# Copying a pass's results aside with GpSimd and storing them at the start of the next pass, in a softmax-times-V kernel

## The chip, the cores and the metric

The kernel runs on one core of one Trainium2 chip. The metric is the device time of one execution in microseconds (us), lower is better. The engines of the core are called PE (matrix multiplication; PEld is its loading of weights), DVE (VectorE), ACT (ScalarE), POOL (GpSimd) and SP (which here only issues the DMA transfers).

## The reference

For 8 x 12 = 96 heads of 1024 x 1024 scores and a 1024 x 64 matrix V, in float32:

```python
def reference(scores: np.ndarray, v: np.ndarray) -> np.ndarray:
    scores_max = np.max(scores, axis=-1, keepdims=True)
    attn = np.exp(scores - scores_max)
    attn = attn / (np.sum(attn, axis=-1, keepdims=True) + 1e-8)
    return np.matmul(attn, v).astype(np.float32)
```

The scores are 403 MB; V and the result are 25.2 MB each.

## The kernel before, in words

One loop runs over the 96 heads in 24 **passes** of four heads (`n0` = 0, 4, ... 92; below, pass p has n0 = 4p). A pass has two **halves**, k = 0 and k = 1, of two heads each. The body of the loop is written out once and used by all passes, with branches (`tc.If`) for the last three.

**A half.** The scores of two heads lie in `s_bufs[k]`: 128 partitions, 16 rows of 1024 scores on each, 8.39 MB. There are two such buffers, one for each half. The 16 rows are worked off in eight **turns** of two rows. ACT takes the exponential of two rows into one of the buffers `p_nat` (float16, L384; eight buffers). No maximum is subtracted; what that needs is verified on the side (`seen`, `watch_v`, `fold`, `judge`). PE transposes each row in eight 128 x 128 blocks into `psT` (L397, two buffers). DVE copies them to `pt` (L409 for two rows at once, L405 for one row in the turns called `late`: the second half of half 1). PE multiplies `pt` by `vones`, which is V with columns of ones (L152, eight products for a row), so that the sums of the softmax come out beside the products. After each three rows DVE takes the reciprocals (L132) and writes the scaled results to `out_bufs[k]` (L140). `in_line` fixes the order on PE: the products of a row follow the transposes of the row three later.

**End of a pass.** `fold` (two small DVE reductions, L284 and L285) reads the whole row of `seen`, in which the reciprocals and the result of `watch_v` lie. `watch_v` is one ACT instruction over the 1 MB of V of the next pass (L266); it writes one column of `seen`, and as a by-product `p_bufs[0]`. `spread_v` (POOL, L255, eight casts for each half) fills `vones` of one half from `v_sb`.

**The queue of transfers.** All transfers are issued by SP, and `queue` chains them, so that they are issued in the order of the program. In the passes 0 to 20 the order is: the load of half 0 of the next pass (`load_first`, issued when ACT has finished half 0), the store of half 0's results (`store(n0, 0)`, 0.52 MB), the load of half 1 of the next pass (when ACT has finished half 1), the store of half 1's results, the load of V for the pass after the next (1.05 MB). In the passes 21 and 22 the loads of scores are cut into parts, each issued when its own rows are free: (4, 6, 6) rows for half 0, and for half 1 (4, 4, 4), then the store of half 1, then (2, 1, 1). In pass 23 nothing is loaded; `end` stores half 1 in two pieces.

**How transfers report.** The build gives the transfers of the loop's body eight semaphores in turn, here called lanes 0 to 7 (`DMAHW0` to `DMAHW7`). Since all passes share one body, both sides of a branch count each lane up by the same amount, and a wait names a lane and a count.

Of the kernel before, what the change touches and what calls it, by code (L numbers as in the profile page):

```python
# [8 lines left out]
FP32 = mybir.dt.float32  # L9
FP16 = mybir.dt.float16  # L10
# [16 lines left out]
def kernel(  # L27
# [6 lines left out]
    nc = tc.nc  # L34
    P = 128

    B, H, SQ, SK = scores.shape
    Bv, Hv, SKv, D = v.shape
    assert (B, H, SK) == (Bv, Hv, SKv)
    BH = B * H  # L40
    assert SQ % P == 0 and SK % P == 0
    C = SK // P
    EB = 2
    G = 3
    LAG = 3
    AHEAD = 4
# [6 lines left out]
    T = 2  # L53
    K = AHEAD // T
    W = P // T
    R = SQ // W
# [8 lines left out]
    out_rows = out.rearrange("b h (j r) d -> (b h j) (r d)", j=W)  # L65

    const_pool = ctx.enter_context(tc.tile_pool(name="const", bufs=1))
    sb_pool = ctx.enter_context(tc.tile_pool(name="sbpool", bufs=1))
# [10 lines left out]
    def buffers(pool, count, shape, dtype, name):  # L79
        return [pool.tile(shape, dtype, name=f"{name}{k}") for k in range(count)]  # L80

    s_bufs = buffers(sb_pool, K, [P, R, SK], FP32, "s_nat")
    v_sb = sb_pool.tile([P, C // L, S, L, D], FP32, name="v_sb")
    p_bufs = buffers(sb_pool, 8, [P, EB, SK], FP16, "p_nat")
    pt_bufs = buffers(sb_pool, 2, [P, EB, SK], FP16, "pt")
    out_bufs = buffers(sb_pool, K, [P, R, D], FP32, "out_sb")
    small_pool = ctx.enter_context(tc.tile_pool(name="small", bufs=1))
    seen = small_pool.tile([P, 1 + K * R + 2], FP32, name="seen")
    nc.gpsimd.memset(seen, 1.0)
# [1 line left out]


    psO_bufs = buffers(ps_pool, 4, [P, 512], FP32, "psO")
    turn = {}

    def take(bufs):
        k = turn.get(id(bufs), 0)
        turn[id(bufs)] = k + 1
        return bufs[k % len(bufs)]

    pending = []
    queued = []
    line = []

    def after(a, b):

        tc.add_manual_dep(
            a.ins,
            b.ins.name,
            mybir.DependencyInfo(mybir.DependencyClass.NoSync, mybir.DependencyReason.DATA),  # L110
            reason="order",
        )

    def in_line(op):

        if line:
            after(op, line[-1])
        line.append(op)

    def queue(dma):  # L120

        if queued:
            after(dma, queued[-1])
        queued.append(dma)
# [37 lines left out]
        if r == R - 1 and k < K - 1:  # L162
            spread_v(k)

    def store(n0, k):

        to = out_rows.rearrange("(m x) y -> m x y", x=P)[bass.ds((n0 + T * k) // T, 1)]
        to = to.rearrange("o x y -> (o x) y")
        send(nc.sync.dma_start(out=to, in_=out_bufs[k][:].rearrange("x r d -> x (r d)")))

    def send(dma):
        for other in stores:
            apart(dma, other)
            apart(other, dma)
        apart(dma, dma)
        stores.append(dma)
        queue(dma)

    def end():

        cut = (GROUPS - 2) * G
        for a, b in ((0, cut), (cut, R)):
            send(
                nc.sync.dma_start(
                    out=out_rows[(BH - T) * W : BH * W, a * D : b * D],
                    in_=out_bufs[K - 1][:, a:b].rearrange("x r d -> x (r d)"),
                )
            )

# [3 lines left out]
    def apart(a, b, reason="stores of two heads are disjoint"):  # L193
        tc.declare_no_dep(a.ins, b.ins, across_iterations=True, reason=reason)
# [18 lines left out]
    def load(k, n, parts=(R,), r=0, **cond):  # L213
        rows_n = sc_rows[bass.ds(n // T, 1)].rearrange("o x r k -> (o x) r k")
        for rows in parts:
            queue(
                nc.sync.dma_start(  # L217
                    out=s_bufs[k][:, r : r + rows, :], in_=rows_n[:, r : r + rows, :], **cond
                )
            )  # L220
            r += rows

    def branch_at(op):

        after(op, line[-1])

    def load_first(n0):

        before = queued[-1:]
        n = (n0 + AHEAD) % BH  # L230
        with tc.If(n0 < BH - 3 * AHEAD) as cmp:
            load(0, n)
            branch_at(queued[-1])
        with cmp.Else():
            queued[:] = before
            load(0, n, (4, 6, 6), cond=(n0 < BH - AHEAD))
            branch_at(queued[-1])
        line.append(queued[-1])

    def load_v(n, **cond):  # L240

# [9 lines left out]
    def spread_v(k):  # L251

        for t in range(T):
            for s in range(S):
                nc.gpsimd.tensor_copy(  # L255
                    out=vones[s * Q : (s + 1) * Q, k, :, t, 0:D].rearrange(
                        "i (h l) d -> i h l d", l=L
                    ),
                    in_=v_sb[(k * T + t) * Q : (k * T + t + 1) * Q, :, s],
                )  # L260

    def watch_v():


        junk = p_bufs[0][:].rearrange("p r k -> p (r k)")
        return nc.scalar.activation(  # L266
            out=junk,
            in_=v_sb[:].rearrange("p h s l d -> p (h s l d)"),
            func=mybir.ActivationFunctionType.Abs,
            scale=1.0 / SUM_MAX,  # L270
            accum_out=seen[:, K * R + 1 : K * R + 2],
        )
# [78 lines left out]
    def last(n0, bank):  # L351

        before = queued[-1:]
        k = K - 1
        with tc.If(n0 < BH - AHEAD) as cmp:
            spread_v(k)
            n = (n0 + AHEAD + T * k) % BH
            with tc.If(n0 < BH - 3 * AHEAD) as cmp2:
                queued[:] = before
                load(k, n)  # L360
                store(n0, k)
                load_v((n0 + 2 * AHEAD) % BH)
            with cmp2.Else():
                queued[:] = before
                load(k, n, (4, 4, 4))
                store(n0, k)
                load(k, n, (2, 1, 1), 12)
                load_v(BH - AHEAD, cond=(n0 < BH - 2 * AHEAD))
        with cmp.Else():
            queued[:] = before  # L370
            end()
            judge(bank)

    def heads(n0):

        for k in range(K):
            st = dict(psO=[take(psO_bufs) for g in range(GROUPS)])
            for r in range(R):
                late = k == K - 1 and r >= R // 2
                if r % EB == 0:  # L380
                    p_nat, psT2, pt2 = take(p_bufs), take(psT_bufs), take(pt_bufs)
                    rows = 1 if late else EB
                    for g in range(0, EB, rows):
                        exp = nc.scalar.activation(  # L384
                            out=p_nat[:, g : g + rows, :].rearrange(
                                "p r (x v) -> p x r v", v=Q * L
                            ),
                            in_=s_bufs[k][:, r + g : r + g + rows, :].rearrange(
                                "p r (i x l) -> p x (r i) l", i=Q, l=L
                            ),  # L390
                            func=EXP,
                        )
                        rewrite(p_nat, exp)
                p_row = p_nat[:, r % EB, :].rearrange("p (h q l) -> p h l q", q=P, l=L)
                psT, pt = psT2[:, r % EB, :], pt2[:, r % EB, :]
                for c in range(C):
                    turned = nc.tensor.transpose(  # L397
                        out=psT[:, c * P : (c + 1) * P],
                        in_=p_row[:, c // L, c % L, :],
                        identity=ident16[:],  # L400
                    )
                    in_line(turned)
                    other_bank(psT2, r % EB, turned)
                if late:
                    copy = nc.vector.tensor_copy(out=pt, in_=psT)  # L405
                    rewrite(pt2, copy)
                    other_bank(psT2, r % EB, copy)
                elif r % EB == EB - 1:
                    copy = nc.vector.tensor_copy(out=pt2[:], in_=psT2[:])  # L409
                    rewrite(pt2, copy)  # L410
                if r == 6 and k == K - 1:
                    load_first(n0)
                    store(n0, 0)
                if r == 13 and k == K - 1:
                    with tc.If(n0 < BH - AHEAD):
                        watch = watch_v()
                        branch_at(watch)
                    line.append(watch)
                pending.append((n0, k, r, pt, st))
                while len(pending) > (LAG - 1 if late and r >= R - EB else LAG):  # L420
                    finish(pending.pop(0))
        while pending:
            finish(pending.pop(0))
        fold()
        last(n0, st["psO"][-1])
# [52 lines left out]
```

## Time and profile before

| | |
|---|---|
| three runs | 1065.42, 1064.98, 1064.54 us (median 1064.98) |
| the profiled execution | 1065.58 us |
| its span, from first to last instruction | 1063.8 us |
| busy, share of the span | PE 77%, PEld 74%, ACT 71%, DVE 66%, POOL 22% |
| DMA queue | 99.1% of the 16 engines' span; 453 MB at a mean of 426 GB/s |
| granted PE clock, mean | 0.875 |

The profiled execution took 1.78 us more than its span, and 0.60 us more than the median of the three runs. In the lists of groups and waits a row names a line of the kernel, an engine, what it writes and reads, and times; "A <- B: x, n, y" in the list of waits means that A waited for B x us in total, n times, at the longest y. In the timeline a row has the start in us from the start of the span, the length, the engine, the line and the instruction, and in brackets how long the engine had been idle and what ended that.

### The profile page before, as it was taken

How to read it: one execution, taken by the hardware profiler on the slowest of the kernel's cores; microseconds unless marked ns; L12 is line 12 of the kernel's file. 1: busy time of each engine (PE TensorE's matmuls, PEld its weight loads, DVE VectorE, ACT ScalarE, POOL GpSimd, SP SyncE). 2: the span in 40 equal slices, each digit the busy share in tenths (PEclk: the TensorE clock that was granted, in tenths of full speed). 3: DMA queues.
4: the chain of work that ended last, by engine and by line, in shares of the span. 5: the costliest groups of instructions: out<-in, count | busy, mean ns of one | idle time of the engine just before them, and what ended most of it. 6: DMA issues, size and time to landing. Idle time of an engine off the chain costs nothing. (4 is left out here: it accounts for less than half of the span.)

```text
span 1063.8 us, 33293 instructions
## 1 busy us (share of the span) xinstructions
PE 814.6 (77%) x12289; PEld 790.1 (74%) x12289; DVE 706.8 (66%) x1395; ACT 754.3 (71%) x530; POOL 239.0 (22%) x400
## 2 busy tenths in 40 slices
PE   2588778886877768886788778886788868887967
PEld 2488767786877768886777778876787867777967
DVE  1467766776667757676577765776667756677858
ACT  4477577776777667766777577775777667768965
POOL 3031130211312113112031130311312113112131
PEclk9788988888898978899888887998888898988989
DMA  9999999999999999999999999999999999999995
GB/s 394 435 429 431 414 434 453 414 453 430 418 453 414 432 455 414 453 414 432 452 416 451 407 443 451 416 448 427 426 448 419 423 437 441 414 453 413 430 415 228
DMA packets 19587, 453.04 MB, mean 426 GB/s; under 512 B 2176, under 2 KB 2304, under 8 KB 8960
## 3 DMA queue, kind: packets, MB, share of 16 engines
q1 hardware_dynamic: 19584, 452.99, 99.1%
q8 instruction: 3, 0.05, 0.0%
HBM read 437.26 MB, written 25.17 MB: 435 GB/s over the span
## 5 line engine op out<-in xcount | busy, mean ns | idle before, releaser
L384 ACT ACTIVATE p_nat<-s_nat 128x2048 f16<-128x2048 f32 (+1 forms) x480 | 707.1, 1557 | 292.5 <-DMA s_nat<-in_scores_dram 278.5
L397 PE MATMUL psT<-ident,p_nat 128*128 128x128 f16 x6144 | 525.5, 238 | 215.5 <-ACT p_nat L384 213.4
L397 PEld LDWEIGHTS <-p_nat 128*128 128x128 f16 x6144 | 442.3, 120 | 227.4 <-ACT p_nat L384 226.2
L409 DVE COPY pt<-psT 128x2048 f16<-128x2048 f16 x288 | 352.4, 1224 | 319.0 <-PE L152 159.0
L152 PE MATMUL psO<-vones,pt 128*128 128x130 f16 x6144 | 504.6, 229 | 28.4 <-DVE pt L405 17.7
L152 PEld LDWEIGHTS <-pt 128*128 128x128 f16 x6144 | 408.0, 102 | 40.7 <-DVE pt L405 21.9
L255 POOL CAST vones<-v_sb 32x512 f16<-32x512 f32 x392 | 238.1, 607 | 811.6 <-PE psT L397 360.9
L140 DVE TENSOR_TENSOR out_sb<-psO,seen 64x192 f32<-64x192 f32 (+1 forms) x576 | 192.0, 333 | 22.7 <-DMA out_dram<-out_sb 3.9
L405 DVE COPY pt<-psT 128x1024 f16<-128x1024 f16 x192 | 123.5, 684 | 2.3
L132 DVE RECIPROCAL seen<-psO 128x3 f32<-128x3 f32 (+1 forms) x288 | 49.6, 172 | 8.5 <-PE L397 4.7
L266 ACT ACTIVATE p_nat<-v_sb 128x2048 f16<-128x2048 f32 x24 | 45.6, 1900 | 1.0 <-DMA v_sb<-in_v_dram 1.0
L266 ACT ACT_TABLE_LOAD x1 | 1.3, 1283 | 5.8 <-DMA v_sb<-in_v_dram 5.8
L284 DVE TENSOR_REDUCE seen<-seen 128x1 f32<-128x34 f32 x24 | 4.5, 188 | 0.8
L266 ACT ACTIVATION_READ_ACCUMULATOR p_nat<-v_sb 128x1 f32 x24 | 4.5, 188 | 0.0
L285 DVE TENSOR_REDUCE seen<-seen 128x1 f32<-128x34 f32 x24 | 4.3, 178 | 0.0
L301 PEld LDWEIGHTS <-right 128*1 128x1 f16 x1 | 0.1, 79 | 1.8 <-DVE right L296 1.8
L301 PE MATMUL psO<-vones,right 128*1 128x1 f16 x1 | 0.2, 164 | 1.6 <-DVE right L296 1.6
L305 DVE CAST count<-psO 1x1 int32<-1x1 f32 x1 | 0.1, 147 | 0.3 <-PE psO L301 0.3
masks.py:199 POOL TENSOR_SCALAR_AFFINE_SELECT ident<-ident 128x128 f32<-128x128 f32 x1 | 0.3, 292 | 0.1
L74 ACT CAST ident<-ident 128x128 f16<-128x128 f32 x1 | 0.3, 282 | 0.0
masks.py:197 POOL MEMSET ident<- 128x128 f32 x1 | 0.2, 204 | 0.3 <-POOLq L462 0.3
L296 DVE SCALAR_TENSOR_TENSOR right<-seen,part 128x1 f16<-128x1 f32 x1 | 0.2, 161 | 0.0
(7 smaller groups left out, 0.8 us busy)
## 6 DMA issues: line engine op xcount, KB each, us to landing
v_sb<-in_v_dram SPq DMA_DIRECT2D x25, 1024.0 KB, 20.3
out_dram<-out_sb SPq DMA_DIRECT2D x47, 512.0 KB, 22.7
s_nat<-in_scores_dram SPq DMA_DIRECT2D x9, 2048.0 KB, 25.9
s_nat<-in_scores_dram SPq DMA_DIRECT2D x6, 3072.0 KB
s_nat<-in_scores_dram SPq DMA_DIRECT2D x2, 4096.0 KB, 18.7
s_nat<-in_scores_dram SPq DMA_DIRECT2D x2, 1024.0 KB
s_nat<-in_scores_dram SPq DMA_DIRECT2D x4, 512.0 KB
s_nat<-in_scores_dram SPq DMA_DIRECT2D x43, 28.4
```

The source lines that it names most:

```text
L132: nc.vector.reciprocal(out=recip, in_=psO[:, :, D : D + 1])
L140: nc.vector.tensor_tensor(out=out_bufs[k][part, g * G : g * G + rows, :], in0=psO[part, :, t * N : t * N + D], in1=recip[part].to_broadcas ...
L152: product = nc.tensor.matmul(out=st["psO"][g][:, i * M : (i + 1) * M], lhsT=pt[:, c * P : (c + 1) * P], rhs=vones[:, k, c].rearrange("p t ...
L255: nc.gpsimd.tensor_copy(out=vones[s * Q : (s + 1) * Q, k, :, t, 0:D].rearrange("i (h l) d -> i h l d", l=L), in_=v_sb[(k * T + t) * Q : (k ...
L266: return nc.scalar.activation(out=junk, in_=v_sb[:].rearrange("p h s l d -> p (h s l d)"), func=mybir.ActivationFunctionType.Abs, scale=1. ...
L284: nc.vector.tensor_reduce(out=seen[:, 0:1], in_=seen[:, 0 : n + 1], axis=X, op=ALU.min)
L285: nc.vector.tensor_reduce(out=seen[:, n + 1 : n + 2], in_=seen[:, 1 : n + 2], axis=X, op=ALU.max)
L301: nc.tensor.matmul(out=cell, lhsT=right[:], rhs=vones[:, 0, 0, 0, D : D + 1], start=True, stop=True)
L384: exp = nc.scalar.activation(out=p_nat[:, g : g + rows, :].rearrange("p r (x v) -> p x r v", v=Q * L), in_=s_bufs[k][:, r + g : r + g + ro ...
L397: turned = nc.tensor.transpose(out=psT[:, c * P : (c + 1) * P], in_=p_row[:, c // L, c % L, :], identity=ident16[:],)
L405: copy = nc.vector.tensor_copy(out=pt, in_=psT)
L409: copy = nc.vector.tensor_copy(out=pt2[:], in_=psT2[:])
```

## The change

- Two new buffers `done` of the size of `out_bufs`; to make room, `p_nat` has six buffers and not eight.
- At the end of a pass POOL copies both `out_bufs` to `done` (`put_by`), behind `spread_v(1)`.
- The two stores of a pass move to the start of the next pass, ahead of its loads (`store_before`). They read `done`. In pass 0 they are skipped.
- `load_first` moves from turn 6 of half 1 to the end of half 0 in the text, and the manual orders on its branch are gone. In the passes 21 and 22 the parts are (4, 4, 4, 4) and (4, 4, 2, 2, 2, 2) rows.
- `watch_v` moves from row 13 of half 1 to the end of the pass, behind `fold` and `spread_v(1)`.
- `end` stores half 0 as well as the two pieces of half 1.
- `late` covers the last four rows of half 1, and not the last eight.

```diff
-    p_bufs = buffers(sb_pool, 8, [P, EB, SK], FP16, "p_nat")
+    p_bufs = buffers(sb_pool, 6, [P, EB, SK], FP16, "p_nat")
...
+    done_bufs = buffers(sb_pool, K, [P, R, D], FP32, "done")
...
+    for done in done_bufs:
+        nc.vector.memset(done, 0.0)
...
-    def store(n0, k):
...
+    def put_by(k):
+
+        nc.gpsimd.tensor_copy(out=done_bufs[k][:], in_=out_bufs[k][:])
+
+    def store_before(n0):
+
+        for k in range(K):
+            n = (n0 + (BH - AHEAD + T * k)) % BH
+            to = out_rows.rearrange("(m x) y -> m x y", x=P)[bass.ds(n // T, 1)]
+            send(
+                nc.sync.dma_start(
+                    out=to.rearrange("o x y -> (o x) y"),
+                    in_=done_bufs[k][:].rearrange("x r d -> x (r d)"),
+                    cond=(n0 > 0),
+                )
+            )
...
         cut = (GROUPS - 2) * G
-        for a, b in ((0, cut), (cut, R)):
+        for k, a, b in ((0, 0, R), (1, 0, cut), (1, cut, R)):
+            n = BH - AHEAD + T * k
...
         with tc.If(n0 < BH - 3 * AHEAD) as cmp:
             load(0, n)
-            branch_at(queued[-1])
         with cmp.Else():
             queued[:] = before
-            load(0, n, (4, 6, 6), cond=(n0 < BH - AHEAD))
-            branch_at(queued[-1])
-        line.append(queued[-1])
+            load(0, n, (4, 4, 4, 4), cond=(n0 < BH - AHEAD))
...
         with tc.If(n0 < BH - AHEAD) as cmp:
             spread_v(k)
+            watch_v()
+            for j in range(K):
+                put_by(j)
...
                 load(k, n)
-                store(n0, k)
                 load_v((n0 + 2 * AHEAD) % BH)
...
-                load(k, n, (4, 4, 4))
-                store(n0, k)
-                load(k, n, (2, 1, 1), 12)
+                load(k, n, (4, 4, 2, 2, 2, 2))
...
     def heads(n0):
 
+        store_before(n0)
         for k in range(K):
...
-                late = k == K - 1 and r >= R // 2
+                late = k == K - 1 and r >= R - 4
...
-                if r == 6 and k == K - 1:
+                if r == R - 1 and k < K - 1:
                     load_first(n0)
-                    store(n0, 0)
-                if r == 13 and k == K - 1:
-                    with tc.If(n0 < BH - AHEAD):
-                        watch = watch_v()
-                        branch_at(watch)
-                    line.append(watch)
```

In the changed kernel the lines have other numbers: the exponentials are L393, the copies L418 and L414, the scaled results L143, `fold` L292 and L293, `watch_v` L274, `spread_v` L263, `put_by` L170, the stores L178 (`store_before`) and L199 (`end`), the loads L232 and L252.

More of the change, by code (lines that the diff above doesn't have):

```diff
@@ L163, in finish @@
             spread_v(k)
-    def store(n0, k):
-        to = out_rows.rearrange("(m x) y -> m x y", x=P)[bass.ds((n0 + T * k) // T, 1)]
-        to = to.rearrange("o x y -> (o x) y")
-        send(nc.sync.dma_start(out=to, in_=out_bufs[k][:].rearrange("x r d -> x (r d)")))
+    def put_by(k):
[11 more added lines that the diff above has]
+            )
     def send(dma):
@@ L181, in end @@
         cut = (GROUPS - 2) * G
-        for a, b in ((0, cut), (cut, R)):
+        for k, a, b in ((0, 0, R), (1, 0, cut), (1, cut, R)):
+            n = BH - AHEAD + T * k
             send(
                 nc.sync.dma_start(
-                    out=out_rows[(BH - T) * W : BH * W, a * D : b * D],
-                    in_=out_bufs[K - 1][:, a:b].rearrange("x r d -> x (r d)"),
+                    out=out_rows[n * W : (n + T) * W, a * D : b * D],
+                    in_=out_bufs[k][:, a:b].rearrange("x r d -> x (r d)"),
                 )
@@ L221, in load @@
             r += rows
-    def branch_at(op):
-        after(op, line[-1])
     def load_first(n0):
@@ L265, in watch_v @@
         junk = p_bufs[0][:].rearrange("p r k -> p (r k)")
-        return nc.scalar.activation(
+        nc.scalar.activation(
             out=junk,
```

## The prediction

> **What bounds the kernel now.** I read the page first, for its row on the DMA engines, then the list of waits:
>
> ```profile
> DMA  9999999999999999999999999999999999999995
> ```
>
> ```profile
> ACT p_nat L384 <- DMA s_nat<-in_scores_dram: 278.5, 46, 13.4
> ...
> DVE out_sb L140 <- DMA out_dram<-out_sb: 3.9, 1, 3.9
> ```
>
> The queue of transfers is full until the last slice, and ACT waits for scores 46 times: the transfers pace the 24 passes. Half 0 of the passes 20 and 21 starts at 897.45 and 941.04, so a pass takes 43.6 us. Half 1 of pass 21 starts at 961.65 (below), 20.6 us after half 0, in which one half (8.39 MB) and one store (0.52 MB) move: a half takes 19.4 us, a store 1.21, V 2.42. The bytes don't change, so a change can gain at the two ends only, or lose by making the engines slower than the queue. So the third view is the chain that ended last, in order of time:
>
> ```profile
> 1009.21 22.03 DMA out_dram<-out_sb
> 1032.11 1.24 DVE pt L409
> 1033.39 1.05 PE psO L152 x8
> ```
>
> In pass 23 DVE may not overwrite `out_sb` before the store of pass 22 has landed; that is the wait of 3.9 us above. The fourth view is the timeline of ACT and DVE in the passes 21 to 23:
>
> ```profile
> 941.04 5.52 ACT L384 ACTIVATE p_nat<-s_nat 128x2048 f16<-128x2048 f32 x3 [6.17 <-DMA s_nat<-in_scores_dram]
> ...
> 944.93 1.23 DVE L409 COPY pt<-psT 128x2048 f16<-128x2048 f16 x1 [4.89 <-PE L397]
> ...
> 961.65 14.91 ACT L384 ACTIVATE p_nat<-s_nat 128x2048 f16<-128x2048 f32 x12 [6.08 <-DMA s_nat<-in_scores_dram]
> 976.46 1.90 ACT L266 ACTIVATE p_nat<-v_sb 128x2048 f16<-128x2048 f32 x1
> ```
>
> ```profile
> 983.94 0.18 DVE L285 TENSOR_REDUCE seen<-seen 128x1 f32<-128x34 f32 x1
> 985.11 2.36 DVE L409 COPY pt<-psT 128x2048 f16<-128x2048 f16 x2 [0.98 <-PE L397]
> ...
> 989.94 0.74 DVE L140 TENSOR_TENSOR out_sb<-psO,seen 64x192 f32<-64x192 f32 x2
> ...
> 1016.96 0.18 DVE L285 TENSOR_REDUCE seen<-seen 128x1 f32<-128x34 f32 x1
> ```
>
> ```profile
> 1059.37 0.18 DVE L285 TENSOR_REDUCE seen<-seen 128x1 f32<-128x34 f32 x1
> ```
>
> Pass 22 shows what a pass takes when its scores are there: 31.9 us of DVE from the first copy to the end of `fold`, 27.2 from the first L140. At 43.6 us a pass has some 11 us to spare.
>
> **The change, part by part.** Two waits of the changed build matter; these are rows of its instruction order (lane 6 is `DMAHW6`, long lists of waits are shortened here):
>
> ```
> 14 L143 TensorTensor out_sb0_84<-psO0_95,seen_91 64x192 [waits DMAHW6, DVE, Pool]
> 32 L232 DMACopy s_nat_74<-in_scores_dram 128x16384 [waits DMAHW6, ..., Activation, ...]
> 44 L274 Activation p_nat0_76,seen_91<-v_sb_75 128x2048 [waits DVE, PE, DMAHW4, Activation, ...]
> 58 L199 DMACopy out_dram<-out_sb_84 128x1024 [waits DMAHW6, DVE]
> ```
>
> *Lane 6.* `end` now stores `out_sb0` (row 58, lane 6), so the loop's first write of `out_sb0` (row 14) waits until all of lane 6 of the pass before has landed. That store runs in pass 23 alone. In all others lane 6 carries the load of half 1 (row 32). So in each pass DVE may write its first result of half 0 only when the scores of half 1 have landed. On DVE all later copies to `pt` stand behind it; PE stops some rows later for want of them. ACT goes on, since six `p_nat` buffers and what PE has taken cover the eight turns of half 0. In the kernel before the lanes of `end` guard `out_sb1`, which is written after those scores have been used anyway.
>
> *`watch_v` behind `fold`.* It writes a column of `seen` that `fold` reads, so it waits for `fold` of its own pass (its count is that of DVE's last instruction). The first exponential of the next pass stands behind it on ACT. From 976.46 to the next exponential at 978.61 are 2.15 us, from the first exponential of a pass to the first copy 3.89 (941.04 to 944.93): `fold` to first copy is 6.15 us with 0.1 for the semaphore, where the kernel before took 0.99 in pass 22.
>
> *Passes 1 to 20.* Let A be the landing of half 1. DVE is let go at A and has 27.1 us of work left (27.2, less 0.1 for two turns copied whole: one copy of 1.23 for two of 0.68, which overlap by 0.08). PE idles while DVE is held, and then restarts at half clock; in pass 17 the granted clock was 0.50 until 5 us after the restart, and a row of transposes and products takes 1.70 us there (745.69 to 747.39) and not 0.91 (752.13 to 753.04). That costs PE up to 2.3 us, DVE nothing to all of it. I take 0.6, since DVE is the slower of the two and has copies in hand: A + 27.7. ACT starts the next pass at A + 29.95 and ends half 0 at A + 44.5 (eight exponentials take 14.5), 0.9 us after the next landing A + 43.6. Then the load of half 0 is issued; the queue still holds V and two stores, 4.84 us. With a start of at most 1.5 us (the last piece of the result, 128 KB, lands 1.9 us after its issue) 2.4 us are left. So the queue stays full and the passes still take 43.6: nothing lost, with 2.4 us of cover. Two passes close that loop, so each us beyond it would cost 0.5 a pass, some 10 in all.
>
> *The end.* Here there is no more cover. Ahead of half 1 of pass 21 one store less is queued: A = 961.65 - 1.2 = 960.4. `fold` of pass 21 ends at 960.4 + 27.7 = 988.1. Pass 22: 6.15 + 31.8 = 37.95, to 1026.05. Lane 6 then carries the first four rows of half 1; they land at 960.4 + 4.84 + 24.2 = 989.4, ahead of the first L143 at 999. Pass 23: again 37.95, to 1064.0. Its last scores land at 960.4 + 87.2 = 1047.6, ahead of their turn at about 1056, so here the loads no longer matter. From the end of `fold` (1059.55) to the end of the span are 4.25 us: 1068.25, against 1063.8, so +4.45. On the profiled execution's 1065.58 that is 1070.0, on the median 1069.4. Bounds: each of the two last passes 0.4 us shorter (the half clock hidden) to 1.4 longer, the first term -0.6 to +1.7: 1067.5 to 1074.
>
> A rule of the Trainium skill bears on the restarts. In this trace PE's last product of pass 16 starts at 764.09 and is issued within 0.65 us, and these slices show the clock down in the third us after it:
>
> ```profile
> 764.00:765.00 1.00, 0.64 (x8) 0.46 (x8) 0.90 (x5) 0.00 (x0) 0.10 (x1) 1.00 0.80 328
> ...
> 766.00:767.00 1.00, 0.00 (x0) 0.00 (x0) 0.00 (x0) 0.31 (x1) 0.88 (x3) 0.89 0.17 70
> 767.00:768.00 1.00, 0.00 (x0) 0.00 (x0) 0.00 (x0) 1.00 (x1) 0.94 (x2) 0.50 2.34 1012
> ```
>
> The Trainium skill, "TensorE: Matmul & The Clock Gate", part 1, gives the cold state after at least one idle window of about 3.4 us, on a grid that runs freely. By that rule the PE gap before pass 22 and pass 23, some 5.4 us (1.2 ahead of `fold`'s end, 2.25 to the first exponential, 1.95 for it), would hold a whole idle window in six cases of ten, and the sum would be an estimated 1 us lower; the trace disagrees, since the clock fell some 2.2 us into a gap, and the measurement decides.
>
> *Edits costed at nothing.* `put_by` and the casts: POOL starts 1.2 us ahead of `fold`'s end, eight casts take 5.3 (0.607 each), two copies of 1024 elements 1.2 to 2.6 (the cast has 512): done 5.3 to 6.7 us after `fold`. The first L143 that waits for it comes 11 us after `fold`; without that cover it costs 2.6 a pass at the end. The two stores wait for POOL on SP; behind them stands the load of half 0, due 16.7 us after `fold`. In pass 22 they also wait for lanes 0 and 1, parts of half 1 that land at 996.7 and 999.1, with V and more parts still queued. Memsets: DVE is idle until 20.8. Six `p_nat` buffers: ACT leads PE by three turns at most where nothing is held. The skipped transfers and the smaller parts have the slack of 1047.6 to 1056. The stall of 3.9 us and the 2.4 us of two stores behind the last loads are gained, but the end no longer waits for them.
>
> **The rivals.**
> *Faster: neither wait holds anything.* It decides at the first L143 of a pass: if lane 6 is long complete there and `fold` early, the last scores set the end: 1047.6, 1.9 of ACT for two rows, and 10.2 from the last exponential (1053.58) to the end: 1059.7, as a time 1061.5. For it: the spare 11 us. Against: the count in the build. 0.05.
> *The same: only `watch_v` waits.* `fold` of pass 21 comes 22.3 us after A (22.5 in the profile, 961.65 to 984.12): 982.7 + 75.9 + 4.25 = 1062.85, as a time 1064.6. It needs lane 6 to be harmless. 0.10.
> *Slower still: the queue runs dry.* If the held half costs 3.5 us more than taken, (3.5 - 2.4) x 0.5 x 20 = 11, and 3.5 at the end: 1084. Against: the clock's price above. 0.05.
>
> **How the numbers follow.** My case has 0.80; its likeliest time is 1069.5, between the two sums. A measurement of this kernel can tell 0.2% (2.1 us) from no change. Faster is the first rival, 0.05; within 0.2% are the second and a few hundredths of my case's lower edge, 0.12; slower 0.83. The range 1065.5 to 1076 holds my case and its bounds; it leaves out the first and the third rival and most of the second, less than 0.2 together.
>
> **What would show it.** Right: a wait of DVE L143 for the load of `s_nat` in nearly every pass, some 3 us each, and one of ACT L274 for DVE L293; half 0 starting 30 us after half 1 and no longer at a landing; DMA still 9s to slice 38; the last 75 us at 38 a pass. Wrong: no wait at L143, DMA slices under 9 in the middle, or ACT waiting for scores in pass 23.

## The result, and the profile after

The changed kernel takes 1094.39 us (median of six runs, 1091.46 to 1099.66), the kernel before on the same chip 1065.2 (1064.54 to 1066.14): a ratio of 1.0279, 95% interval 1.0252 to 1.0307. It is slower, as forecast, but by 29 us and not by 4.5. Its profiled execution is the slowest of the six: 1099.66 us, span 1097.9.

The page's rows on the DMA engines, first of the changed kernel, then of the kernel before (which had 99.1% for the queue):

```profile
DMA  9999999999999999999999999999999999999992
GB/s 420 417 440 404 447 427 404 417 409 415 427 427 404 451 420 425 427 411 427 418 425 399 406 454 415 412 428 415 432 411 397 438 396 439 401 400 435 429 427 107
...
q1 hardware_dynamic: 19872, 452.99, 97.7%
```

```profile
GB/s 394 435 429 431 414 434 453 414 453 430 418 453 414 432 455 414 453 414 432 452 416 451 407 443 451 416 448 427 426 448 419 423 437 441 414 453 413 430 415 228
```

The engines still look busy: 9s to slice 38, as the prediction wanted. But they move less: a mean of 413 GB/s against 426. "Busy" counts the time that packets take, and it does not tell whether a packet takes longer than it must.

Both forecast waits are there, in the list of waits of the changed kernel (`A <- B: us, times, longest`; L363 is the branch behind `fold`), and ACT hardly waits for scores any more (278.5 us, 46 times before). A wait at L143 is 5.1 us long on average, where some 3 were expected:

```profile
ACT p_nat L274 <- DVEq L363: 288.8, 23, 13.5
...
DVE out_sb L143 <- DMA s_nat<-in_scores_dram: 107.6, 21, 7.5
...
ACT p_nat L393 <- DMA s_nat<-in_scores_dram: 20.1, 8, 13.5
```

A pass in the middle of the run, in the timelines of DVE, ACT and SP:

```profile
743.23 0.18 DVE L293 TENSOR_REDUCE seen<-seen 128x1 f32<-128x34 f32 x1
749.66 1.22 DVE L418 COPY pt<-psT 128x2048 f16<-128x2048 f16 x1 [6.25 <-PE L406]
...
760.44 0.74 DVE L143 TENSOR_TENSOR out_sb<-psO,seen 64x192 f32<-64x192 f32 x2 [5.54 <-DMA s_nat<-in_scores_dram]
...
788.63 0.18 DVE L293 TENSOR_REDUCE seen<-seen 128x1 f32<-128x34 f32 x1
```

```profile
743.60 1.91 ACT L274 ACTIVATE p_nat<-v_sb 128x2048 f16<-128x2048 f32 x1 [13.44 <-DVEq L363]
745.41 0.19 ACT L274 ACTIVATION_READ_ACCUMULATOR p_nat<-v_sb 128x1 f32 x1
745.76 29.69 ACT L393 ACTIVATE p_nat<-s_nat 128x2048 f16<-128x2048 f32 x18 [0.16 <-issue]
```

```profile
747.80 0.34 SPq L252 DMA_DIRECT2D v_sb<-in_v_dram  x1
750.48 1.20 SPq L178 DMA_DIRECT2D out_dram<-done  x2
760.48 0.35 SPq L232 DMA_DIRECT2D s_nat<-in_scores_dram  x1
```

DVE is held 5.54 us, until half 1 lands (A, here 760.3; in the pass before 714.7). `fold` ends 28.4 us after the release. `watch_v` follows it, and the load of half 0 is issued at 760.48, at the landing. The pass takes 45.6 us from landing to landing. All of this is the forecast chain, except for the length of the pass, which was to be 43.6.

The trace also holds every packet that the 16 DMA engines moved. A packet of scores (65536 bytes) takes a mean of 2.440 us here and 2.421 before; a packet of 8192 bytes (V, and a few of the last scores) 0.364 and 0.313. In the changed kernel 23% of the latter take more than 0.32 us, most of these 0.32 to 0.7. The time that all packets take grows by 19.0 us per engine, over half of the 34.1 us by which the span has grown.

### The profile page after: what moved, and what is told of

Same layout as the page of the kernel before. It is cut to its first block, busy times and chain, and to the rows that moved or that the text cites. A ratio compares the mean times of both kernels' runs of the same rounds, so it can differ in the third digit from the quotient of the medians.

```text
span 1097.9 us, 32453 instructions
## 1 busy us (share of the span) xinstructions
PE 804.7 (73%) x12289; PEld 776.2 (71%) x12289; DVE 703.7 (64%) x1349; ACT 753.2 (69%) x482; POOL 286.5 (26%) x446
## 5 line engine op out<-in xcount | busy, mean ns | idle before, releaser
L393 ACT ACTIVATE p_nat<-s_nat 128x2048 f16<-128x2048 f32 (+1 forms) x432 | 703.7, 1709 | 39.0 <-DMA s_nat<-in_scores_dram 20.1
L406 PE MATMUL psT<-ident,p_nat 128*128 128x128 f16 x6144 | 515.3, 235 | 158.0 <-ACT p_nat L393 158.0
L155 PE MATMUL psO<-vones,pt 128*128 128x130 f16 x6144 | 499.2, 227 | 129.8 <-DVE pt L418 112.9
L418 DVE COPY pt<-psT 128x2048 f16<-128x2048 f16 x336 | 411.2, 1224 | 254.5 <-PE L406 161.6
L406 PEld LDWEIGHTS <-p_nat 128*128 128x128 f16 x6144 | 435.5, 120 | 166.3 <-ACT p_nat L393 166.3
L155 PEld LDWEIGHTS <-pt 128*128 128x128 f16 x6144 | 400.3, 101 | 149.8 <-DVE pt L418 131.4
L263 POOL CAST vones<-v_sb 32x512 f16<-32x512 f32 x392 | 239.2, 610 | 793.7 <-PE psT L406 561.7
L143 DVE TENSOR_TENSOR out_sb<-psO,seen 64x192 f32<-64x192 f32 (+1 forms) x576 | 191.9, 333 | 127.1 <-DMA s_nat<-in_scores_dram 107.6
L274 ACT ACTIVATE p_nat<-v_sb 128x2048 f16<-128x2048 f32 x24 | 45.8, 1909 | 288.8 <-DVEq L363 288.8
L414 DVE COPY pt<-psT 128x1024 f16<-128x1024 f16 x96 | 63.4, 681 | 1.5
L170 POOL COPY done<-out_sb 128x1024 f32<-128x1024 f32 x46 | 46.5, 1036 | 2.8
L292 DVE TENSOR_REDUCE seen<-seen 128x1 f32<-128x34 f32 x24 | 4.5, 189 | 0.8
L274 ACT ACTIVATION_READ_ACCUMULATOR p_nat<-v_sb 128x1 f32 x24 | 4.5, 187 | 0.0
L293 DVE TENSOR_REDUCE seen<-seen 128x1 f32<-128x34 f32 x24 | 4.3, 178 | 0.0
```

What stands on the lines that cost most here:

```text
L143: nc.vector.tensor_tensor(out=out_bufs[k][part, g * G : g * G + rows, :], in0=psO[part, :, t * N : t * N + D], in1=recip[part].to_broadcas ...
L155: product = nc.tensor.matmul(out=st["psO"][g][:, i * M : (i + 1) * M], lhsT=pt[:, c * P : (c + 1) * P], rhs=vones[:, k, c].rearrange("p t ...
L170: nc.gpsimd.tensor_copy(out=done_bufs[k][:], in_=out_bufs[k][:])
L263: nc.gpsimd.tensor_copy(out=vones[s * Q : (s + 1) * Q, k, :, t, 0:D].rearrange("i (h l) d -> i h l d", l=L), in_=v_sb[(k * T + t) * Q : (k ...
L274: nc.scalar.activation(out=junk, in_=v_sb[:].rearrange("p h s l d -> p (h s l d)"), func=mybir.ActivationFunctionType.Abs, scale=1.0 / SUM ...
L292: nc.vector.tensor_reduce(out=seen[:, 0:1], in_=seen[:, 0 : n + 1], axis=X, op=ALU.min)
```

## The experiments

All times below are medians beside runs of the kernel before on the same chip (1065.5 to 1065.7); the interval is that of the ratio.

**Which wait, or both.** Three kernels undo one wait, the other, and both; copies, stores, parts and `late` stay as the change has them. `lane_free`:

```diff
             queued[:] = before
+            put_by(0)
             end()
...
-                    in_=out_bufs[k][:, a:b].rearrange("x r d -> x (r d)"),
+                    in_=(out_bufs if k else done_bufs)[k][:, a:b].rearrange("x r d -> x (r d)"),
```

`watch_back`; `both_free` has both edits:

```diff
             spread_v(k)
-            watch_v()
...
+                if r == 13 and k == K - 1:
+                    with tc.If(n0 < BH - AHEAD):
+                        watch_v()
```

> Pass 23 copies half 0's results to done as well and stores them from there, so out_sb0 is read by no transfer and DVE is never held for the load of half 1; watch_v still stands behind fold. Theory 1 (the two waits add up, the load of half 0 is issued too late, and the queue of transfers runs dry): fold comes 22.3 us after the landing of half 1 instead of 27.7, the load of half 0 is issued 5.4 us earlier, the queue stays full (98.5% or more of the span), and the end is that of the second rival, 1062 to 1066 us. Theory 2 (watch_v behind fold alone empties the queue): above 1080. Theory 3 (the stores in their new place, or POOL's copies, make the packets slower): above 1080.

> watch_v is back at row 13 of half 1; DVE is still held for the load of half 1. Theory 1: ACT starts half 0 some 2 to 5 us earlier, which is more than the queue lacks; DMA at 98.5% or more, and at the end fold of pass 21 at 988.1 plus two passes of 32.8 us is earlier than the last scores plus 12.1 (1059.7) allow: 1061 to 1068 us. Theory 2 (watch_v alone): the same 1061 to 1068, so this run tells theory 2 apart only together with lane_free. Theory 3: above 1080.

> Both waits are undone, all else of the change stays (copies by POOL, stores at the start of the next pass, parts, late). Theories 1 and 2: 1060 to 1064 us, the first rival's sum of 1061.5, which is faster than before; the packets of V back at 0.31 us mean. Theory 3: above 1080, since copies and stores are where the change put them.

Measured: `lane_free` 1066.9 us (1.0005 to 1.0023), `watch_back` 1068.2 (1.0017 to 1.0035), `both_free` 1061.1 (0.9948 to 0.9975, which is faster than before). Either wait alone leaves the queue as full as it was, and the last rows of the queue say so: 99.0, 98.8 and 99.4%. Both together cost 33 us, each alone 6 to 7. So theory 2 (one wait) and theory 3 (stores or copies) fall: all three kernels have the stores and the copies, and in none of them is the queue less full. `lane_free` and `watch_back` come out just above the ranges expected of them (1062 to 1066, 1061 to 1068). The page of `both_free`:

```profile
GB/s 396 437 436 428 407 464 428 431 428 413 438 436 436 436 434 437 436 436 436 436 436 431 413 448 426 431 426 430 441 436 436 436 415 456 436 436 404 426 434 289
...
q1 hardware_dynamic: 19872, 452.99, 99.4%
```

The 6 to 7 us of the single waits arise at the end. `lane_free` needs 39.7 and 38.7 us for the last two passes, `both_free` 33.8 and 38.9. `watch_back` needs 34.3 and 39.0, but `fold` of pass 21 ends 6.6 us later than in `both_free`, and the held write strikes once more in pass 23, where lane 6 carries the first four rows of half 1; from there to the end of `fold` are 28.5 us:

```profile
1033.68 0.74 DVE L143 TENSOR_TENSOR out_sb<-psO,seen 64x192 f32<-64x192 f32 x2 [3.66 <-DMA s_nat<-in_scores_dram]
```

**Both waits kept, the load issued earlier.** In the passes 0 to 20:

```diff
-            load(0, n)
+            load(0, n, (R // 2, R // 2))
```

> The changed kernel with both waits kept; in the passes 0 to 20 the load of half 0 is cut into two of 8 rows, the first issued when ACT has finished four of the eight exponentials, 7 us earlier. Theory 1: the queue never runs dry, a pass takes 43.6 us again and what is left is the end as forecast: 1067 to 1074 us; waits of DVE L143 for the scores and of ACT for fold are still there, about as long. Theory 2 the same. Theory 3, or a delay that acts by another way than the empty queue: above 1085.

Measured: 1073.7 us (1.0064 to 1.0092). The waits stand as they were (DVE L143 87.3 us in 21 times, ACT L274 274.5 in 23), a pass takes 43.63 us, and a packet of V 0.315. One edit that touches neither wait brings back 20.7 of the 29 us. So most of what the two waits cost, they cost by making the load late.

With the cut at 14 and 2 rows the first part is issued only 1.8 us earlier. Theory 1 has two forms from here on, which the text on `hold_0` below spells out: 1a has the cover as the prediction reckoned it, and 1b has it end at an issue of about A - 1.1.

```diff
-            load(0, n)
+            load(0, n, (14, 2))
```

> The changed kernel with both waits; in the passes 0 to 20 the load of half 0 is cut into 14 and 2 rows, so the first is issued 1.8 us earlier than the whole was (two_loads_8_8: 7 us earlier, 1073.7 us). Theory 1b: the loss goes from 1.0 us a pass to 0.25 (half of what the issue is still late, since two passes close the loop): 1076 to 1083. Theory 1a: as the changed kernel or as two_loads_8_8, 1073 to 1075. If the time of issue does not matter but the size of a load does: 1085 or more.

Measured: 1083.7 us (1.0150 to 1.0184), just above theory 1b's range: some passes lose time and some don't (44.1 us a pass on average).

**How late is too late.** Three kernels move only the time of issue, in `both_free`, where ACT, PE and DVE have time to spare. One ACT instruction that reads both halves stands ahead of half 1's first exponential (`hold_0`), behind the first (`hold_1`) or behind the second (`hold_2`); the load of half 0 waits for it:

```diff
+    def hold():
+        nc.scalar.activation(
+            out=held, in_=s_bufs[0][:, R - 1, 0:1],
+            func=mybir.ActivationFunctionType.Identity, bias=s_bufs[1][:, 0, 0:1],
+        )
...
+            if k == K - 1:
+                hold()
+                load_first(n0)
             for r in range(R):
...
-                if r == R - 1 and k < K - 1:
-                    load_first(n0)
```

> both_free, in which one ACT instruction of one element reads half 0's and half 1's scores ahead of half 1's first exponential, so that in the passes 0 to 20 the load of half 0 is issued some 0.4 us after the landing of half 1 (A) and not 4.8 us before it; ACT, PE and DVE have their 11 us of slack as in both_free (1061.06). Theory 1a (cover as the prediction reckoned it: the queue lasts until an issue at A + 2.4): 1061 to 1063 us. Theory 1b (what the changed kernel and two_loads_8_8 together give: its issue stands at A, and it loses 1.0 us a pass, so the cover ends at an issue of about A - 1.1): 1.5 us x 20 passes, 1088 to 1094 us, with 8192-byte packets slowed from 0.315 to about 0.36 us as in the changed kernel. Theory 4 (the loss in the changed kernel comes of held DVE and PE, not of the time of issue): 1061 to 1063.

> The same with the instruction behind half 1's first exponential: issue at about A + 2.3. Theory 1a: still 1061 to 1063. Theory 1b: 3.4 us x 20, 1125 to 1133. Theory 4: 1061 to 1063.

> The same behind half 1's second exponential: issue at about A + 4.2. Theory 1a: (4.2 - 2.4) x 20 = 36, 1097. Theory 1b: 5.3 us x 20, 1163 to 1171. Theory 4: 1061 to 1065. Between the three runs theory 1b wants 19 us for each us of delay.

Measured: 1084.7 (1.0153 to 1.0187), 1098.9 (1.0292 to 1.0327) and 1114.3 us (1.0426 to 1.0472). Theory 4 (held engines) and theory 1a (cover to A + 2.4) fall with `hold_0`: nothing is held there but the load. It loses 1.2 us a pass with the issue 0.6 us after the landing:

```profile
715.90 0.29 ACT L386 ACTIVATE held<-s_nat,s_nat 128x1 f32<-128x1 f32 x1 [5.50 <-DMA s_nat<-in_scores_dram]
716.10 14.69 ACT L405 ACTIVATE p_nat<-s_nat 128x2048 f16<-128x2048 f32 x10
```

```profile
716.39 0.36 SPq L232 DMA_DIRECT2D s_nat<-in_scores_dram  x1
```

Theory 1b had the threshold about right and the slope wrong: it wanted 19 us for each us of delay, and the runs give 7.8 and 8.5; all three times lie below its ranges.

**A smaller delay.** Two ACT instructions of 1.9 us in the same place, which wait for nothing:

```diff
+    def hold():
+        for j in (4, 3):
+            nc.scalar.activation(
+                out=p_bufs[j][:].rearrange("p r k -> p (r k)"),
+                in_=s_bufs[0][:, R - EB : R, :].rearrange("p r k -> p (r k)"),
+                func=mybir.ActivationFunctionType.Abs,
+                scale=1.0 / SUM_MAX,
+            )
```

> both_free with two ACT instructions of 1.9 us each (Abs of half 0's last rows into p_nat buffers that are free) between half 0's last exponential and half 1's first: in the passes 0 to 20 the load of half 0 is issued 1.0 us before the landing of half 1 (A) instead of 4.8. Theory 5 (the engine that is furthest ahead counts: it starts V 2.8 us before A, has 4.95 us of V and stores, and the load needs up to 1.9 us from issue to its first packets, so the limit is an issue at A + 0.2; hold_0, at A + 0.4, was over it): no loss, 1061 to 1063 us, 8192-byte packets at 0.315 us. Theory 1b (loss from A - 1.1 on, growing): 1062 to 1066 with slower packets. If every us of delay costs the same, on the line from hold_0 to hold_2 (7.5 us of time for each us): about 1074.

Measured: 1064.2 us (0.9979 to 0.9998). The time alone would also fit theory 1b (1062 to 1066), but that wanted slower packets, and there are none: 8192 bytes take 0.311 us. The passes lose next to nothing (43.60 us); in all twenty the queue falls 1.4 us behind that of `both_free`. The rest arises in pass 23, where the added instructions run too: it takes 41.8 us from `fold` to `fold`, and 38.9 in `both_free`. Theory 5's range left that out.

The series together, from the packets and landings of each trace. "Issue" is the median time of the load of half 0 (of its first part) against the landing of half 1 (A); "a pass" is a mean over 18 passes, between the landings of the engine that is done first; "slow V" and "slow scores" are what packets took beyond 0.309 us for 8192 bytes, 2.4175 for 65536 and 2.116 for 57344, per engine and pass:

| kernel | issue | a pass | slow V | slow scores | time |
|---|---|---|---|---|---|
| both_free | A - 4.5 | 43.59 | 0.00 | 0.01 | 1061.1 |
| lane_free | A - 4.3 | 43.59 | 0.00 | 0.01 | 1066.9 |
| hold_minus_1 | A - 0.9 | 43.60 | 0.00 | 0.03 | 1064.2 |
| two_loads_14_2 | A - 0.7 (-2.4 to 1.4) | 44.13 | 0.29 | 0.17 | 1083.7 |
| hold_0 | A + 0.6 | 44.77 | 0.75 | 0.33 | 1084.7 |
| changed kernel | A + 1.0 (-1.2 to 2.9) | 44.91 | 0.62 | 0.39 | 1094.4 |
| hold_1 | A + 2.4 | 45.32 | 0.89 | 0.54 | 1098.9 |
| hold_2 | A + 4.2 | 46.01 | 0.96 | 0.70 | 1114.3 |

Between A - 0.9 and A + 0.6 the passes go from losing nothing to losing 1.2 us. In `hold_0` and the changed kernel slow packets make 1.0 to 1.1 us of a pass's loss of 1.2 to 1.3; only in `hold_2` is there much idle time besides (0.8 us).

The two kernels whose issue moves from pass to pass say the same within one trace. In the changed kernel V is slow (0.6 to 1.2 us per engine) behind each of the 13 passes that issued the load at A + 0.17 or later, and not slow (0.13 at most) behind each of the six that issued it at A + 0.14 or earlier. In `two_loads_14_2` no V is slow behind the ten issues at A - 0.7 or earlier, and behind eight of the nine later ones V is slow by 0.2 to 1.2 us. So one issue in time ends the disturbance.

**Best version.** `both_free`, 1061.1 us, is faster than both kernels: 0.4% faster than before, 3.0% faster than the changed kernel.

## Why the prediction was right and wrong

- *The order of cases.* Slower was right, and both waits stand in the trace where the build's counts put them. The size was far off, beyond the range of 1065.5 to 1076, and most of the loss came by a way that the prediction held to be covered, the queue; only the smaller part came by the end, from which it had forecast slower.
- *Bounds of the kernel.* Right for passes whose queue is full: 43.6 us a pass before, in `both_free` and in both single-wait kernels.
- *Lane 6 and `watch_v`.* Right, with small errors. From `fold` to the first copy 6.25 us (forecast 6.15); from the landing to the end of `fold` a median of 28.7 (27.7); the end of half 0 on ACT, and with it the issue, 45.8 us after the landing (44.5).
- *Passes 1 to 20: this step failed.* It put the last harmless issue at A + 3.3 (0.9 plus 2.4 of cover). The runs put it between A - 0.9 and A + 0.6, and the passes of the changed kernel at about A + 0.15. The chain was also 1.3 us later than forecast, but by the prediction's own limit that would have been harmless. What failed is the term "the queue still holds V and two stores, 4.84 us" counted from A. A landing is the signal of the last of 16 engines. In the trace the first engine is 2.5 to 2.6 us ahead of the last in every whole load of half 1 in the kernel before, and 2.4 to 2.9 in `both_free`, `lane_free` and `two_loads_8_8`: about one packet of scores. In `both_free` it starts V 2.8 us ahead of A, so it has V and the stores (4.95 us) done at A + 2.2, and a load's first packets come 1.0 us after its issue, the last engine's 1.9 (in `hold_2`, where nearly all engines were idle at the issue). By this sum, an estimate, the limit is an issue at A + 0.3 to A + 1.2, and up to 0.6 us earlier where the first engine is further ahead (it starts V 3.4 us ahead of A in the changed kernel). The start of at most 1.5 us was nearly right; the spread, which stood in the records of the trace before, was not looked at.
- *What lateness costs.* The prediction took 0.5 us a pass for each us, as idle time. The loss has a jump instead: with the issue at A + 0.6 packets slow down, which costs 1.2 us a pass at once, and then 0.3 to 0.4 for each further us. The late issue is shown to be the cause. That it acts by the first engines running dry is the likely reading, and it is not shown: behind three passes (one of the changed kernel, two of `hold_0`) V was slow by 0.7 to 0.9 us, although around their issue the 16 engines together stood idle for some 0.1 us at most.
- *The end.* The last two passes took 39.1 and 38.5 us (forecast 37.95 each, bounds -0.4 to +1.4). With the queue full and both waits there (`two_loads_8_8`) the kernel takes 1073.7. Its profiled execution is 4.6 us above the 1070.0 forecast for one: 0.9 in the landing of pass 21 (961.3 against 960.4), 1.0 from there to its `fold`, 2.5 in the two passes (38.7 and 39.7), 0.1 behind them. The time is inside the bounds given, 1067.5 to 1074; the last pass alone is beyond its own.
- *The sum.* So of the 24.9 us between forecast and result 20.7 belong to the queue and 4.2 to the chain of the end.
- *The clock's rule.* By the rule of the Trainium skill, "TensorE: Matmul & The Clock Gate", part 1, the sum would have been an estimated 1 us lower. In the gap before pass 23 PE's last product is issued by 1053.6 and the clock falls within the slice 1055 to 1056, 1.4 to 2.4 us later; it stays at 0.50 until 1062, 2.6 us after the restart. In the gap before pass 22 it fell 3.4 us after (1014.6 to 1018). So in one of the two gaps the clock fell sooner than after an idle window of that rule, about 3.4 us. In both the restart was at half clock, and both passes came out longer than forecast, not shorter. The stretches of 1 us (clock, DMA share and GB/s last) speak for the dearer term:

```profile
1053.00:1054.00 1.00, 0.63 (x8) 0.46 (x8) 0.93 (x4) 0.00 (x0) 0.00 (x0) 1.00 1.11 475
...
1055.00:1056.00 1.00, 0.00 (x0) 0.00 (x0) 0.13 (x2) 0.68 (x1) 0.94 (x2) 0.77 1.03 442
1056.00:1057.00 1.00, 0.00 (x0) 0.00 (x0) 0.00 (x0) 1.00 (x1) 0.88 (x3) 0.50 1.11 475
...
1059.00:1060.00 1.00, 0.56 (x6) 0.56 (x7) 0.00 (x0) 1.00 (x2) 0.88 (x2) 0.50 1.07 459
```

- *Edits at nothing.* Right. `put_by` takes 2.02 us a pass, inside its bounds:

```profile
793.19 2.02 POOL L170 COPY done<-out_sb 128x1024 f32<-128x1024 f32 x2
```

- *Slips in the working.* The first copy to the end of `fold` in pass 22 is 32.0 us (985.11 to 1017.14) and not 31.9. The rows of 1.70 and 0.91 us at 745.69 and 752.13 are of half 1 of pass 16, and not of pass 17, whose clock stands beside them. Neither changes the result.
- *The rivals.* "Neither wait" gave 1061.5; `both_free` measured 1061.1. "Only `watch_v`" gave 1064.6; `lane_free` measured 1066.9, since the last two passes took 39.7 and 38.7 us and not 38 each. "The queue runs dry" was the right rival with too small a price: 1084 by 3.5 us of lateness. It was given 0.05 because its condition was compared with 2.4 us of cover, and that cover did not exist; the chain was 1.3 us late, and that was enough.

## What to carry to other kernels

When a queue of transfers is the bound, count its cover from the engine that is furthest ahead, not from the landing, which is the slowest engine's; the spread of the 16 stands in the trace of the kernel before. A load that is issued only just too late may cost more than its lateness (here 1.2 us a pass), so a margin that nothing visible needs is worth keeping; cutting a load so that its first part can be issued earlier buys it cheaply. And a transfer that runs in one pass alone can put its lane's wait into every pass of a loop that shares one body.

## What was not expected of the hardware

The 16 engines fall into a pattern of their own and keep it. In `both_free` V's packets are slow once, in the load of V for the third pass (1.00 us per engine); from the next pass on every pass repeats the one before within 0.1 us, and hardly any packet is slow (0.01 us a pass). The first engine stays one packet of scores ahead of the last. When the load is issued too late the pattern is lost, and the next V is slow; where the issue is late in most passes, as in the changed kernel, V is slow in most of them (13 of 19).

Why the packets take longer is open. The Trainium skill, "DMA: Bandwidth & Descriptors", in the section on the descriptor swizzle, states that in a transfer over 128 partitions each engine writes one port of the SBUF, the same in each such transfer; by that, engines out of step would not meet in the SBUF. No run here shows whether that holds, or separates the memory's side from the SBUF's, and why V's small packets suffer most was not tried.
